# Mixture-of-experts stage: four split buffers in place of three, and a first gather in two steps

## The chip, the cores and the metric

The kernel runs on one core of one Trainium2 chip. The metric is the device time of one execution in microseconds (us), lower being better. Before the change the median of three runs is 1938.57 us (1936.62 to 1939.97).

## The reference, cut to what matters

Two layers of a hybrid backbone are computed for 256 latent tokens of width 1024 (and 256 context tokens). The change lies in the last part of the second layer: the output projection of its mixer, the router, and eight experts of which each token uses two.

```python
def moe_swiglu(xs, router_w, router_b, w_gate, w_up, w_down):
    logits = xs @ router_w + router_b
    top_val, top_idx = lax.top_k(logits, TOP_K)
    top_p = jax.nn.softmax(top_val, axis=-1)
    gates = jnp.sum(jax.nn.one_hot(top_idx, N_EXPERTS) * top_p[..., None], axis=-2)
    y = jnp.zeros_like(xs)
    for e in range(N_EXPERTS):
        y = y + gates[..., e:e + 1] * swiglu(xs, w_gate[e], w_up[e], w_down[e])
    return y
...
def swiglu(xs, w_gate, w_up, w_down):
    return (jax.nn.silu(xs @ w_gate) * (xs @ w_up)) @ w_down
```

D_MODEL is 1024, D_EXPERT 2816, N_EXPERTS 8 and TOP_K 2. The arithmetic is float32.

## The kernel before, in words

**Weights in two parts.** A float32 weight is used as the sum of a rounded part `hi` and a rest `lo`, each of a type that TensorE (PE) multiplies in one pass. A weight tile is 128 x 2048 numbers, 1 MB. The sync engine's queue (SP, L214) loads it into a buffer `raw`; ScalarE (ACT, L635) writes `hi` from it; VectorE (DVE, L636) writes `lo` as the difference; then PE multiplies with both. The three pools are opened by `open_ring` (L206, called at L1703): six buffers for `raw`, three for `hi`, three for `lo`. A buffer of `raw` is free when its `lo` is written, one of `hi` or `lo` when PE has read it.

**Experts.** The router sorts the experts by their number of tokens. Four of them (position 0 to 3) get 128 slots and are called big here, four get 64 slots and are called small; `order` in `experts` (L1503) takes big and small in turn. Each expert has 33 tiles: 11 of `m_gate`, 11 of `m_up`, 11 of `m_down`, in all 264 tiles. `expert_up` (L1586) goes through gate and up in six pieces of 512 hidden columns (the last 256). For a big expert each piece of a tile takes three matmuls (L1603, L1604, L1606); then come `h` (ACT L1632, DVE L1633), transposes (PE L1635) and `hT` (ACT L1639, DVE L1640). A small expert has the two halves of its input side by side in 128 columns, so two matmuls do (L1603, L1604), and sums over the halves (L1615 to L1629: ACT `h`, DVE `u`, PE L1619, ACT `g`, ...). `expert_down` (L1645) of the expert before is woven into the pieces, one tile at a time.

**Gather.** `gather` (L1543) makes the inputs of one big and one small expert at once. DVE writes a table of zeros and ones, `hot` (L1551, four instructions of 128 columns: two token blocks, two experts); PE multiplies the tokens with it (L1561, 32 matmuls of 256 columns, 128 for the big and 128 for the small expert); ACT copies the results of the first 16 (L1569) and DVE those of the other 16 (L1567) into `xghi`, `xglo` and `xs`; PE turns `hot` (L1574) and fetches the gate values (L1579), DVE copies them to `gslot` (L1582). The first gather comes right after the router, the next three at the third piece (`c == 2`) of each small expert. The router's last steps on DVE are the sort (up to L1481), the integers for the addresses of the experts' weights (L1487 to L1494), and the loading of one of them into registers of the engines (L1495).

**Before the router.** `odd_out` (L1187) projects the mixer's output with four tiles of `o_out`. They go through the same three pools, and the first three tiles of the experts are split in the same stage, ahead of need.

**Order.** Every engine works through its own list in the order that the compiled program fixes. So what an engine can do next is set by that list and by the waits of its head.

Of the kernel before, what the change touches and what calls it, by code (L numbers as in the profile page):

```python
# [162 lines left out]
class Kernel:  # L163
# [174 lines left out]

    def ssq_add(self, pool, tag, bank, m, segs, bufs=3, direct=False):
        nc = self.nc  # L340
        n = segs[-1][1]
        sq = pool.tile([P, T], F32, tag=tag, name="nsq", bufs=bufs)[:, :n]
        for a, b, v in segs:
            nc.scalar.activation(sq[:, a:b], v, AF.Square)
        if direct:
            for t in range(n // P):
                nc.tensor.matmul(bank[:, t:t + 1], lhsT=sq[:, t * P:t * P + P], rhs=self.mean_d[:, 0:1],
                                 start=m == 0 and t == 0, stop=m == KD - 1 and t == n // P - 1)
            return
# [837 lines left out]
    def odd_out(self, od):  # L1187
# [5 lines left out]
        cm = self.cm = self.const(self.mp, "moe")  # L1193
        self.sorted = self.mp.tile([P, 6, NE], F32, name="sorted")
        self.ints = self.mp.tile([P, 1 + 2 * NE], I32, name="ints")
        self.y2 = [flat[1][:, i * D:i * D + D] for i in range(2)]
        with ExitStack() as st:
# [28 lines left out]
            def back(m, ps):  # L1226
                r = self.resl[:, m]
                nc.vector.scalar_tensor_tensor(r, ps, mix[2][:, m, 0:1], r, op0=ALU.mult, op1=ALU.add)
                xm = yp.tile([P, L], F32, tag="xg", name="xg", bufs=3)
                nc.scalar.activation(xm, r, AF.Copy, scale=gs[:, m, 0:1])  # L1230
                self.ssq_add(yp, "sq", ssq, m, [(0, L, r)])
# [189 lines left out]
    def route(self, xp, lg, cm, tag):  # L1421
# [33 lines left out]
        for b in range(2):  # L1455
            mm(cnt, lhsT=self.ones, rhs=sel[:, b], start=b == 0, stop=b == 1)
        pg = tile_(6, NE)
        pos = pg[:, 0:2]
# [22 lines left out]
        nc.vector.tensor_reduce(self.sorted, moved, axis=AX.X, op=ALU.add)  # L1481
        self.pos, self.gate = self.sorted[:, 0:2], self.sorted[:, 2:4]
        over = tile_(NE)
        nc.vector.tensor_tensor(over, self.sorted[:, 5], cm["cap"], op=ALU.subtract)
        nc.vector.tensor_scalar(over, over, 0.0, None, op0=ALU.max)
        ints = xp.tile([P, 1 + 2 * NE], I32, name="ints")
        nc.vector.tensor_copy(ints[:, 1:1 + NE], self.sorted[:, 4])  # L1487
# [5 lines left out]
                                         max_val=NE - 1) for i in range(1, NE)]  # L1493
        nc.vector.tensor_copy(self.ints, ints)  # L1494
        self.most = nc.values_load(ints[0:1, 0:1], min_val=0, max_val=L)  # L1495
# [7 lines left out]
    def experts(self, wk):  # L1503
        got = {0: self.gather(wk, self.pos, 0, NB)}
        order = [p + NB * s for p in range(NB) for s in range(2)]
        down, todo = iter(()), None
        for n, p in enumerate(order):
            small, i = divmod(p, NB)
            x, hT = got[i][small], []
            for c, _ in enumerate(self.expert_up(wk, p, x, hT)):  # L1510
                if c == 0 and todo:
                    self.scatter(wk, *todo)
                    todo = None
                if c == 2 and small and i + 1 < NB:
# [12 lines left out]

    def overflow(self, wk):
        with self.tc.If(self.most > 0):
            for p in range(NE):  # L1530
                over = self.nc.values_load(self.ints[0:1, 1 + NE + p:2 + NE + p], min_val=0, max_val=L)
                with self.tc.If(over > 0):
                    pos = wk.tile([P, 2, NE], F32, tag="pos2", name="pos2", bufs=1)
                    self.nc.vector.tensor_scalar(pos, self.pos, float(-P if p < NB else -64), None, op0=ALU.add)
                    x, hT = self.gather(wk, pos, p, None)[0], []
                    for _ in self.expert_up(wk, p, x, hT, False):
                        pass
                    for todo in self.expert_down(wk, p, x, hT, False):
                        pass
                    self.scatter(wk, *todo)  # L1540
            self.finish(wk)

    def gather(self, wk, pos, p, s):  # L1543
        nc = self.nc
        mm = nc.tensor.matmul
        cm = self.cm
        hot = wk.tile([P, 2, 2, P], F32R, tag="hot", name="hot", bufs=2)
        both = [(1, p, "slot")] + ([] if s is None else [(0, s, "slot2")])
        for b in range(2):
            for i, e, slot in both:  # L1550
                nc.vector.tensor_scalar(hot[:, b, i], cm[slot], pos[:, b, e:e + 1], None, op0=ALU.is_equal)  # L1551
        xg = [wk.tile([P, KD, P], F32R, tag="xg" + n, name="xg" + n, bufs=1) for n in ("hi", "lo")]
        xs = None if s is None else wk.tile([P, KD, P], F32R, tag="xs", name="xs", bufs=2)
        cols = slice(0, 2) if xs is not None else slice(1, 2)
        for j, (src, dst) in enumerate(zip((self.thi, self.tlo), xg)):
            for k in range(0, KD, 2):
                ps = self.bank("tr").rearrange("p (k i w) -> p k i w", k=2, i=2)
                for kk in range(2):
                    c = slice((k + kk) * P, (k + kk + 1) * P)
                    for b in range(2):  # L1560
                        mm(ps[:, kk, cols], lhsT=src[:, b, c], rhs=hot[:, b, cols], start=b == 0, stop=b == 1)  # L1561
                parts = [(dst[:, k:k + 2], ps[:, :, 1])]
                if xs is not None:
# [13 lines left out]
        for i, e, _ in both:  # L1577
            for b in range(2):
                mm(ps[:, i:i + 1], lhsT=hot[:, b, i].bitcast(F32), rhs=self.gate[:, b, e:e + 1], start=b == 0,  # L1579
                   stop=b == 1)  # L1580
        gs = wk.tile([P, 2], F32, tag="gslot", name="gslot", bufs=2)
        nc.vector.tensor_copy(gs[:, cols], ps[:, cols])  # L1582
        big = (xg, hotT[:, 1], gs[:, 1:2])
        return [big] if xs is None else [big, ((xs,), hotT[:, 0], gs[:, 0:1])]

    def expert_up(self, wk, p, now, hT, ahead=True):  # L1586
# [4 lines left out]
        for c in range(6):  # L1591
# [21 lines left out]
            if small:  # L1613
                u = wk.tile([P, 512], F32, tag="u", name="u", bufs=2)
                nc.scalar.activation(h[:, :width], pgu[0][:, :width], AF.Copy)  # L1615
                nc.vector.tensor_copy(u[:, :width], pgu[1][:, :width])
                for i, t in enumerate((h, u)):
                    for j in range(n):
                        mm(ps[:, 256 * i + 64 * j:256 * i + 64 * j + 64], lhsT=t[:, j * P:(j + 1) * P],  # L1619
                           rhs=self.cm["sum2"], start=True, stop=True)  # L1620
                g = wk.tile([P, 256], F32, tag="g", name="g", bufs=2)[:, :64 * n]
                nc.scalar.activation(g, ps[:, :64 * n], AF.Silu)
                nc.vector.tensor_tensor(g, g, ps[:, 256:256 + 64 * n], op=ALU.mult)
                if c == 0:
                    self.hS = self.mp.tile([P, FT, 2, 64], F32R, tag="hS", name="hS", bufs=1)
                o = self.hS[:, 4 * c:4 * c + n]
# [58 lines left out]
    def run(self, inject=None):  # L1685
        self.setup()
        self.small = self.ctx.enter_context(self.pool("small"))
        with ExitStack() as st:
# [7 lines left out]
            with ExitStack() as s1:  # L1696
# [32 lines left out]
```

## Time and profile before

| | before |
|---|---|
| median of three runs | 1938.57 us |
| profiled execution, its own time | 1935.74 us |
| span of the profiled execution | 1933.9 us |
| PE busy, share of the span | 1768.6 us, 91% |
| DVE busy | 1445.9 us, 75% |
| ACT busy | 1006.3 us, 52% |
| mean granted clock of TensorE | 0.967 |

The profiled execution took 1.84 us more than its span, from the first to the last instruction. Busy time is a sum over the span; the stages have different limits, and the experts take the part from about 1125 us on. Windows of 198 us, 1392 to 1590 and 1590 to 1788, hold just one pair of experts each.

### The profile page before, as it was taken

How to read it: one execution, taken by the hardware profiler on the slowest of the kernel's cores; microseconds unless marked ns; L12 is line 12 of the kernel's file. 1: busy time of each engine (PE TensorE's matmuls, PEld its weight loads, DVE VectorE, ACT ScalarE, POOL GpSimd, SP SyncE). 2: the span in 40 equal slices, each digit the busy share in tenths (PEclk: the TensorE clock that was granted, in tenths of full speed). 3: DMA queues.
4: the chain of work that ended last, by engine and by line, in shares of the span. 5: the costliest groups of instructions: out<-in, count | busy, mean ns of one | idle time of the engine just before them, and what ended most of it. 6: DMA issues, size and time to landing. Idle time of an engine off the chain costs nothing.

```text
span 1933.9 us, 28843 instructions
## 1 busy us (share of the span) xinstructions
PE 1768.6 (91%) x11628; PEld 1390.4 (72%) x11628; DVE 1445.9 (75%) x1966; ACT 1006.3 (52%) x1131; POOL 90.3 (5%) x92
## 2 busy tenths in 40 slices
PE   6989999698999999989999879989999899998996
PEld 3657776377888888778876768777777677777775
DVE  4577888657995383456685678888888889888987
ACT  3433325635232222366562357776677677767774
POOL 0011102200000000002110000000000000000000
PEclk8999999798999999989999889999999999999997
DMA  7232111325666163123203339999999999989993
GB/s 291 91 111 88 46 42 49 109 88 200 236 238 239 66 223 125 66 80 109 87 23 146 144 133 359 363 344 363 345 341 363 353 346 341 370 335 360 352 380 119
DMA packets 57310, 409.32 MB, mean 212 GB/s; under 512 B 6480, under 2 KB 6864, under 8 KB 8016
## 3 DMA queue, kind: packets, MB, share of 16 engines
q1 hardware_dynamic: 57168, 407.39, 56.5%
q8 instruction: 93, 1.52, 0.3%
q14 instruction: 49, 0.40, 0.1%
HBM read 406.32 MB, written 1.05 MB: 211 GB/s over the span
## 4 chain that ended last, share of the span: by engine, by line
PE 71%; DVE 17%; ACT 7%; issue 4%; POOL 1%; DMA 0%; SPq 0%; DVEq 0%; ACTq 0%; POOLq 0%
DVE lo L636 10%; PE bank_gu L1604 6%; PE bank_b L234 6%; PE bank_b L235 6%; PE bank_b L236 6%; PE bank_gu L1603 5%; ACT hi L635 5%; PE bank_mm L234 4%; PE bank_mm L235 4%; PE bank_mm L236 4%; PE bank_gu L1606 3%; PE bank_dn L1660 3%; PE bank_dn L1659 2%; PE bank_dn L1662 1%; PE bank_tr L1619 1%
## 5 line engine op out<-in xcount | busy, mean ns | idle before, releaser
L636 DVE TENSOR_TENSOR lo<-raw,hi 128x2048 fp32r<-128x2048 f32 (+1 forms) x398 | 765.4, 1946 | 186.3 <-ACT hi L635 184.2
L635 ACT ACTIVATE hi<-raw 128x2048 fp32r<-128x2048 f32 (+1 forms) x398 | 641.3, 1632 | 276.0 <-PE bank_b L235 140.5
L1604 PE MATMUL bank_gu<-lo,xghi 128*128 128x512 f32 (+1 forms) x384 | 148.9, 388 | 27.2 <-DVE lo L636 26.7
L1604 PE MATMUL bank_gu<-lo,xs 128*128 128x512 f32 (+1 forms) x384 | 146.2, 387 | 7.5 <-DVE lo L636 6.4
L1603 PE MATMUL bank_gu<-hi,xghi 128*128 128x512 f32 (+1 forms) x384 | 145.6, 379 | 0.0
L1606 PE MATMUL bank_gu<-hi,xglo 128*128 128x512 f32 (+1 forms) x384 | 144.5, 376 | 0.0
L1603 PE MATMUL bank_gu<-hi,xs 128*128 128x512 f32 (+1 forms) x384 | 144.3, 382 | 0.2
L234 PE MATMUL bank_b<-xhi,hi 128*128 128x512 f32 x352 | 138.0, 394 | 2.9 <-ACT xhi L635 2.9
L234 PE MATMUL bank_mm<-xhi,hi 128*128 128x512 f32 (+1 forms) x320 | 120.9, 380 | 21.5 <-ACT hi L635 15.3
L235 PE MATMUL bank_b<-xlo,hi 128*128 128x512 f32 x352 | 137.9, 392 | 0.0
L236 PE MATMUL bank_b<-xhi,lo 128*128 128x512 f32 x352 | 137.6, 391 | 0.0
L236 PE MATMUL bank_mm<-xhi,lo 128*128 128x512 f32 (+1 forms) x320 | 118.3, 370 | 2.9 <-DVE lo L636 2.1
L235 PE MATMUL bank_mm<-xlo,hi 128*128 128x512 f32 (+1 forms) x320 | 119.7, 374 | 0.0
L1604 PEld LDWEIGHTS bank_gu<-lo,xghi 128*128 128x128 f32 x384 | 72.2, 188 | 54.0 <-DVE lo L636 41.6
L1604 PEld LDWEIGHTS bank_gu<-lo,xs 128*128 128x128 f32 x384 | 72.4, 188 | 32.6 <-DVE lo L636 21.2
L312 DVE SCALAR_TENSOR_TENSOR ada<-ada_raw,sT,ada 128x1024 f32<-128x1024 f32 x70 | 87.2, 1282 | 5.5 <-DMA ada_raw<-in_ada_v 4.8
L234 PEld LDWEIGHTS bank_mm<-xhi,hi 128*128 128x128 f32 x320 | 62.4, 196 | 37.2 <-ACT hi L635 16.5
L1603 PEld LDWEIGHTS bank_gu<-hi,xghi 128*128 128x128 f32 x384 | 72.3, 188 | 13.5
L1603 PEld LDWEIGHTS bank_gu<-hi,xs 128*128 128x128 f32 x384 | 72.4, 188 | 12.4 <-ACT hi L635 1.5
L1606 PEld LDWEIGHTS bank_gu<-hi,xglo 128*128 128x128 f32 x384 | 72.4, 188 | 12.2
L234 PEld LDWEIGHTS bank_b<-xhi,hi 128*128 128x128 f32 x352 | 66.5, 189 | 17.0 <-ACT xhi L635 3.2
L1660 PE MATMUL bank_dn<-lo,hT 128*128 128x512 f32 x176 | 72.8, 414 | 6.2 <-DVE lo L636 6.2
(512 smaller groups left out, 3461.0 us busy)
## 6 DMA issues: line engine op xcount, KB each, us to landing
raw<-in_m_up SPq DMA_DIRECT2D x88, 1024.0 KB, 7.2
raw<-in_m_gate SPq DMA_DIRECT2D x88, 1024.0 KB, 7.1
raw<-in_m_down SPq DMA_DIRECT2D x88, 1024.0 KB, 7.3
ada_raw<-in_ada_v SPq DMA_DIRECT2D x28, 1024.0 KB, 4.9
raw<-in_ada SPq DMA_DIRECT2D x20, 1024.0 KB, 6.0
raw<-in_o_in SPq DMA_DIRECT2D x16, 1024.0 KB, 4.9
raw<-in_w_in SPq DMA_DIRECT2D x12, 1024.0 KB, 4.9
raw<-in_f_gate SPq DMA_DIRECT2D x11, 1024.0 KB, 5.8
```

Of the source, the lines that this page charges most:

```text
L234: mm(out, lhsT=whi, rhs=xhi, start=start, stop=False)
L235: mm(out, lhsT=whi, rhs=xlo, start=False, stop=False)
L236: mm(out, lhsT=wlo, rhs=xhi, start=False, stop=stop)
L312: nc.vector.scalar_tensor_tensor(acc[r], w[:, k], s, acc[r], op0=ALU.mult, op1=ALU.add)
L635: self.nc.scalar.activation(hi, x, AF.Copy)
L636: (self.nc.gpsimd if pool else self.nc.vector).tensor_tensor(lo, x, hi.bitcast(F32), op=ALU.subtract)
L1603: mm(o, lhsT=xg[0][:, kk], rhs=whi(k), start=kk == 0, stop=False)
L1604: mm(o, lhsT=xg[0][:, kk], rhs=wlo(k), start=False, stop=small and kk == 7)
L1606: mm(o, lhsT=xg[1][:, kk], rhs=whi(k), start=False, stop=kk == 7)
L1619: mm(ps[:, 256 * i + 64 * j:256 * i + 64 * j + 64], lhsT=t[:, j * P:(j + 1) * P], rhs=self.cm["sum2"], start=True, stop=True)
L1659: mm(py[a], lhsT=h[0], rhs=whi(i)[:, half[a]], start=f == 0, stop=False)
L1660: mm(py[a], lhsT=h[0], rhs=wlo(i)[:, half[a]], start=False, stop=len(h) == 1 and f == FT - 1)
```

## The change

`open_ring` gets four buffers for `hi` and `lo` in place of three. To make room, several other tiles are taken less often or put elsewhere: `xs` goes into a tile that is no longer needed (`self.x[0]`), `hot`, `u` and `g` get one buffer, and the squares in `ssq_add` get a narrower tile. The first gather is cut in two: one for the first big expert alone, from the places before the sort (`self.plain`), and one for the first small expert from the sorted places. The copy of the integers (L1494 before) goes.

```diff
-    def ssq_add(self, pool, tag, bank, m, segs, bufs=3, direct=False):
+    def ssq_add(self, pool, tag, bank, m, segs, bufs=3, direct=False, width=T):
...
-        sq = pool.tile([P, T], F32, tag=tag, name="nsq", bufs=bufs)[:, :n]
+        sq = pool.tile([P, width], F32, tag=tag, name="nsq", bufs=bufs)[:, :n]
...
+        self.plain = self.mp.tile([P, 6, NE], F32, name="plain")
         self.ints = self.mp.tile([P, 1 + 2 * NE], I32, name="ints")
+        self.xs = [flat[0][:, i * D:i * D + D].rearrange("p (k w) -> p k w", k=KD) for i in range(2)]
...
-        pg = tile_(6, NE)
+        pg = self.plain
...
-        ints = xp.tile([P, 1 + 2 * NE], I32, name="ints")
+        ints = self.ints
...
-        nc.vector.tensor_copy(self.ints, ints)
         self.most = nc.values_load(ints[0:1, 0:1], min_val=0, max_val=L)
...
     def experts(self, wk):
-        got = {0: self.gather(wk, self.pos, 0, NB)}
+        got = {0: self.gather(wk, self.plain, 0, None)}
...
             x, hT = got[i][small], []
+            if n == 0:
+                got[0] += self.gather(wk, self.sorted, None, NB)
...
-                    got[i + 1] = self.gather(wk, self.pos, i + 1, NB + i + 1)
+                    got[i + 1] = self.gather(wk, self.sorted, i + 1, NB + i + 1)
...
-    def gather(self, wk, pos, p, s):
+    def gather(self, wk, places, p, s):
...
-        hot = wk.tile([P, 2, 2, P], F32R, tag="hot", name="hot", bufs=2)
-        both = [(1, p, "slot")] + ([] if s is None else [(0, s, "slot2")])
+        pos, gate = places[:, 0:2], places[:, 2:4]
+        hot = wk.tile([P, 2, 2, P], F32R, tag="hot", name="hot", bufs=1)
+        jobs = [(i, e, slot) for i, e, slot in ((1, p, "slot"), (0, s, "slot2")) if e is not None]
+        cols = slice(jobs[-1][0], jobs[0][0] + 1)
...
-        xs = None if s is None else wk.tile([P, KD, P], F32R, tag="xs", name="xs", bufs=2)
...
+        if s is not None:
+            xs = self.xs[s % 2]
...
-        hotT = wk.tile([P, 2, L], F32R, tag="hotT", name="hotT", bufs=2)
+        hotT = wk.tile([P, 2, L], F32R, tag="hotT", name="hotT", bufs=3)
...
-                u = wk.tile([P, 512], F32, tag="u", name="u", bufs=2)
+                u = wk.tile([P, 512], F32, tag="u", name="u", bufs=1)
...
-                g = wk.tile([P, 256], F32, tag="g", name="g", bufs=2)[:, :64 * n]
+                g = wk.tile([P, 256], F32, tag="g", name="g", bufs=1)[:, :64 * n]
...
-            self.open_ring(st, 6, 3, 2048)
+            self.open_ring(st, 6, 4, 2048)
```

**Steady work, ACT.** In the second big expert ACT's list, from one `hT` to the next, with the events that each instruction waits for (`PE` is a matmul, `DVE` an instruction of DVE, `DMAHW` a load); before:

```order
L1639 ACTIVATE hT_11220<-bank_tr_11326 128x512 [waits PE_49]
L635 ACTIVATE hi_11356<-raw_11354 128x2048 [waits DMAHW5_49,DVE_49]
L635 ACTIVATE hi_11374<-raw_11372 128x2048 [waits DMAHW6_49,DVE_49]
L635 ACTIVATE hi_11389<-raw_11387 128x2048 [waits DMAHW7_49,DVE_49,PE_49]
L1632 ACTIVATE h_11437<-bank_gu_11335 128x512 [waits PE_49]
L635 ACTIVATE hi_11407<-raw_11405 128x2048 [waits DMAHW0_49,DVE_49]
L635 ACTIVATE hi_11425<-raw_11423 128x2048 [waits DMAHW1_49,DVE_49,PE_49]
L635 ACTIVATE hi_11451<-raw_11449 128x2048 [waits DMAHW2_49,DVE_49,PE_49]
L1639 ACTIVATE hT_11445<-bank_tr_11438 128x512 [waits PE_49]
```

After the change the same place reads:

```order
L1649 ACTIVATE hT_11263<-bank_tr_11369 128x512 [waits PE_49]
L635 ACTIVATE hi_11399<-raw_11397 128x2048 [waits DMAHW5_49,DVE_49]
L635 ACTIVATE hi_11417<-raw_11415 128x2048 [waits DMAHW6_49,DVE_49]
L635 ACTIVATE hi_11432<-raw_11430 128x2048 [waits DMAHW7_49,DVE_49]
L1642 ACTIVATE h_11480<-bank_gu_11378 128x512 [waits PE_49]
L635 ACTIVATE hi_11450<-raw_11448 128x2048 [waits DMAHW0_49,DVE_49]
L635 ACTIVATE hi_11468<-raw_11466 128x2048 [waits DMAHW1_49,DVE_49]
L635 ACTIVATE hi_11494<-raw_11492 128x2048 [waits DMAHW2_49,DVE_49,PE_49]
L1649 ACTIVATE hT_11488<-bank_tr_11481 128x512 [waits PE_49]
```

The instructions stand in the same order and the `hi` between two others are of the same tiles; two of the three waits for PE by a `hi` are gone.

**First gather, PE.** From its last transposes on, PE's list before:

```order
L1574 MATMUL bank_tr_9856<-const_base_60,hot_9792 128x128 x3
L1606 MATMUL bank_gu_9870<-hi_9871,xglo_9798 128x512
L1579 MATMUL bank_tr_9863<-sorted_9211,hot_9792 128x1 [waits DVE_49,PE_49]
L1579 MATMUL bank_tr_9863<-sorted_9211,hot_9792 128x1 x3
L1603 MATMUL bank_gu_9870<-hi_9871,xghi_9797 128x512
L1604 MATMUL bank_gu_9870<-lo_9872,xghi_9797 128x512
L1606 MATMUL bank_gu_9870<-hi_9871,xglo_9798 128x512
```

And after, where the lines have moved by 8 to 10:

```order
L1584 MATMUL bank_tr_9843<-const_base_60,hot_9790 128x128
L1613 MATMUL bank_gu_9914<-hi_9915,xghi_9793 128x512
L1614 MATMUL bank_gu_9914<-lo_9916,xghi_9793 128x512
L1589 MATMUL bank_tr_9848<-plain_9212,hot_9790 128x1 [waits DVE_49]
L1589 MATMUL bank_tr_9848<-plain_9212,hot_9790 128x1
L1616 MATMUL bank_gu_9914<-hi_9915,xglo_9794 128x512
L1613 MATMUL bank_gu_9914<-hi_9915,xghi_9793 128x512
L1569 MATMUL bank_tr_9856<-hot_9853,xhi_4458 128x128 [waits DVE_49,Activation_49]
L1569 MATMUL bank_tr_9856<-hot_9853,xhi_4458 128x128 [waits DVE_49]
L1569 MATMUL bank_tr_9856<-hot_9853,xhi_4458 128x128 x2
L1569 MATMUL bank_tr_9862<-hot_9853,xhi_4458 128x128 x4
```

The first gather's 32 matmuls have 128 columns instead of 256, and after only four matmuls of the first gate tile a second run of 32 follows, for the small expert, with a table `hot` that DVE writes in between.

**Output projection, DVE.** What DVE does between the last normalisation of the mixer and the first results of the projection, before:

```order
L636 TENSOR_TENSOR lo_9301<-raw_9297,hi_9300 128x2048
L636 TENSOR_TENSOR lo_9376<-raw_9372,hi_9375 128x2048
L636 TENSOR_TENSOR lo_9452<-raw_9448,hi_9451 128x2048
L1206 TENSOR_TENSOR rwg_9224<-rw_9222,gs_9220 128x64
L1218 TENSOR_TENSOR rbias_9248<-bank_t_9239,par_58 128x8
L626 SCALAR_TENSOR_TENSOR xlo_4459<-bank_t_9250,hg_7054,xhi_4458 128x256
```

After (between the two pieces stand six more `xlo`, L626, without anything among them):

```order
L636 TENSOR_TENSOR lo_9302<-raw_9298,hi_9301 128x2048
L1208 TENSOR_TENSOR rwg_9225<-rw_9223,gs_9221 128x64
L1220 TENSOR_TENSOR rbias_9249<-bank_t_9240,par_58 128x8
L636 TENSOR_TENSOR lo_9377<-raw_9373,hi_9376 128x2048
L626 SCALAR_TENSOR_TENSOR xlo_4459<-bank_t_9251,hg_7054,xhi_4458 128x256
```

```order
L636 TENSOR_TENSOR lo_9453<-raw_9449,hi_9452 128x2048
L626 SCALAR_TENSOR_TENSOR xlo_4459<-bank_t_9286,hg_7054,xhi_4458 128x256
L636 TENSOR_TENSOR lo_9529<-raw_9525,hi_9528 128x2048
L1230 SCALAR_TENSOR_TENSOR resl_84<-bank_mm_9300,vec1_73,resl_84 128x256
```

Two `lo` that stood ahead of `rwg` now stand behind it, the third ahead of the last `xlo`, and the fourth (which stood behind the second `resl`) ahead of the first. Four tiles of the experts are split behind these, where three were; the last of them stands at the place where the last stood before.

## Rows read from the trace of the kernel before

**Rows 1.** The page: header and part 1, busy time.

```profile
span 1933.9 us, 28843 instructions
...
PE 1768.6 (91%) x11628; PEld 1390.4 (72%) x11628; DVE 1445.9 (75%) x1966; ACT 1006.3 (52%) x1131; POOL 90.3 (5%) x92
```

**Rows 2.** Windows: stretch, length, busy by engine, clock, DMA share, GB/s.

```profile
1135.00:1150.00 15.00, 15.00 (x68) 12.02 (x67) 10.62 (x8) 11.82 (x8) 0.00 (x0) 1.00 0.52 179
1150.00:1200.00 50.00, 50.00 (x249) 41.65 (x248) 44.62 (x27) 38.20 (x27) 0.00 (x0) 1.00 0.96 362
...
1392.00:1590.00 198.00, 183.37 (x887) 145.34 (x886) 173.25 (x126) 139.96 (x110) 0.00 (x0) 1.00 0.94 350
```

**Rows 3.** Waits, 1150 to 1934: us in total, times, longest us.

```profile
DVE lo L636 <- ACT hi L635: 72.9, 87, 2.4
...
PE bank_gu L1604 <- DVE lo L636: 33.0, 44, 2.7
...
ACT hi L635 <- PE bank_gu L1606: 25.8, 26, 3.9
...
ACT hi L635 <- PE bank_gu L1603: 11.6, 31, 1.2
```

**Rows 4.** Waits of the load queue, same stretch.

```profile
SPq L214 <- DVE lo L636: 487.4, 200, 6.2
```

**Rows 5.** Timeline of ACT and DVE, a small expert: start, us, engine, operation, idle before.

```profile
1450.64 0.60 ACT L1615 ACTIVATE h<-bank_gu 128x512 f32<-128x512 f32 x1 [1.28 <-PE bank_gu L1604]
1451.13 5.59 ACT L635 ACTIVATE hi<-raw 128x2048 fp32r<-128x2048 f32 x3
...
1453.07 6.70 DVE L636 TENSOR_TENSOR lo<-raw,hi 128x2048 fp32r<-128x2048 f32 x3 [1.35 <-ACT hi L635]
```

**Rows 6.** Timeline of ACT and PE, a big expert.

```profile
1344.94 0.60 ACT L1639 ACTIVATE hT<-bank_tr 128x512 fp32r<-128x512 f32 x1 [3.38 <-PE bank_tr L1635]
1345.44 5.51 ACT L635 ACTIVATE hi<-raw 128x2048 fp32r<-128x2048 f32 x3
...
1349.73 0.50 PE L1604 MATMUL bank_gu<-lo,xghi 128*128 128x512 f32 x1 [1.09 <-DVE lo L636]
```

**Rows 7.** Timeline of ACT and DVE at the last tiles.

```profile
1897.35 3.78 ACT L635 ACTIVATE hi<-raw 128x2048 fp32r<-128x2048 f32 x2 [1.27 <-PE bank_dn L1659]
...
1899.30 2.29 DVE L636 TENSOR_TENSOR lo<-raw,hi 128x2048 fp32r<-128x2048 f32 x1 [0.29 <-ACT hi L635]
```

**Rows 8.** Timeline of DVE and PE at the first gather.

```profile
1123.96 0.18 DVE L1494 COPY ints<-ints 128x17 int32<-128x17 int32 x1
1124.61 1.66 DVE L1551 TENSOR_SCALAR hot<-const_moe,sorted 128x128 fp32r<-128x128 f32 x8 [0.47 <-DVE ints L1494]
1125.24 4.00 PE L1561 MATMUL bank_tr<-hot,xhi 128*128 128x256 f32 x16 [6.46 <-DVE hot L1551]
...
1129.31 1.30 PE L1561 MATMUL bank_tr<-hot,xlo 128*128 128x256 f32 x8
...
1133.09 1.02 PE L1579 MATMUL bank_tr<-sorted,hot 128*128 128x1 f32 x8
```

**Rows 9.** Chain that ended last, a small expert: start, us, what.

```profile
1445.99 0.84 PE bank_tr L1619 x8
```

**Rows 10.** Timeline of DVE, PE and ACT in the output projection.

```profile
1068.01 6.69 DVE L636 TENSOR_TENSOR lo<-raw,hi 128x2048 fp32r<-128x2048 f32 x3
...
1074.97 1.11 PE L623 MATMUL bank_t<-const_base,yo 128*128 128x128 f32 x4 [0.69 <-DVE rbias L1218]
...
1105.34 1.91 ACT L635 ACTIVATE hi<-raw 128x2048 fp32r<-128x2048 f32 x1 [1.31 <-PE bank_mm L235]
...
1107.28 2.29 DVE L636 TENSOR_TENSOR lo<-raw,hi 128x2048 fp32r<-128x2048 f32 x1 [1.34 <-ACT hi L635]
```

**Rows 11.** Timeline of ACT, first small expert, third piece.

```profile
1216.49 0.60 ACT L1615 ACTIVATE h<-bank_gu 128x512 f32<-128x512 f32 x1 [1.08 <-PE bank_gu L1604]
...
1217.40 1.93 ACT L635 ACTIVATE hi<-raw 128x2048 fp32r<-128x2048 f32 x1
```

More of the change, by code (lines that the diff above doesn't have):

```diff
@@ L1230, in back @@
                 nc.scalar.activation(xm, r, AF.Copy, scale=gs[:, m, 0:1])
-                self.ssq_add(yp, "sq", ssq, m, [(0, L, r)])
+                self.ssq_add(yp, "sq", ssq, m, [(0, L, r)], width=L)
                 c = slice(m % 4 * P, m % 4 * P + P)
@@ L1481, in route @@
         nc.vector.tensor_reduce(self.sorted, moved, axis=AX.X, op=ALU.add)
-        self.pos, self.gate = self.sorted[:, 0:2], self.sorted[:, 2:4]
         over = tile_(NE)
@@ L1532, in overflow @@
                 with self.tc.If(over > 0):
-                    pos = wk.tile([P, 2, NE], F32, tag="pos2", name="pos2", bufs=1)
-                    self.nc.vector.tensor_scalar(pos, self.pos, float(-P if p < NB else -64), None, op0=ALU.add)
+                    pos = wk.tile([P, 4, NE], F32, tag="pos2", name="pos2", bufs=1)
+                    self.nc.vector.tensor_scalar(pos[:, 0:2], self.sorted[:, 0:2], float(-P if p < NB else -64), None,
+                                                 op0=ALU.add)
+                    self.nc.vector.tensor_copy(pos[:, 2:4], self.sorted[:, 2:4])
                     x, hT = self.gather(wk, pos, p, None)[0], []
@@ L1546, in gather @@
         cm = self.cm
-        hot = wk.tile([P, 2, 2, P], F32R, tag="hot", name="hot", bufs=2)
-        both = [(1, p, "slot")] + ([] if s is None else [(0, s, "slot2")])
+        pos, gate = places[:, 0:2], places[:, 2:4]
+        hot = wk.tile([P, 2, 2, P], F32R, tag="hot", name="hot", bufs=1)
+        jobs = [(i, e, slot) for i, e, slot in ((1, p, "slot"), (0, s, "slot2")) if e is not None]
+        cols = slice(jobs[-1][0], jobs[0][0] + 1)
         for b in range(2):
-            for i, e, slot in both:
+            for i, e, slot in jobs:
                 nc.vector.tensor_scalar(hot[:, b, i], cm[slot], pos[:, b, e:e + 1], None, op0=ALU.is_equal)
-        xg = [wk.tile([P, KD, P], F32R, tag="xg" + n, name="xg" + n, bufs=1) for n in ("hi", "lo")]
-        xs = None if s is None else wk.tile([P, KD, P], F32R, tag="xs", name="xs", bufs=2)
-        cols = slice(0, 2) if xs is not None else slice(1, 2)
-        for j, (src, dst) in enumerate(zip((self.thi, self.tlo), xg)):
+        xg = xs = None
+        if p is not None:
+            xg = [wk.tile([P, KD, P], F32R, tag="xg" + n, name="xg" + n, bufs=1) for n in ("hi", "lo")]
+        if s is not None:
+            xs = self.xs[s % 2]
+        for j, src in enumerate((self.thi, self.tlo)):
             for k in range(0, KD, 2):
@@ L1561, in gather @@
                         mm(ps[:, kk, cols], lhsT=src[:, b, c], rhs=hot[:, b, cols], start=b == 0, stop=b == 1)
-                parts = [(dst[:, k:k + 2], ps[:, :, 1])]
+                parts = []
+                if xg:
+                    parts.append((xg[j][:, k:k + 2], ps[:, :, 1]))
                 if xs is not None:
@@ L1570, in gather @@
         ps = self.bank("tr").rearrange("p (i b w) -> p i b w", i=2, b=2)
-        hotT = wk.tile([P, 2, L], F32R, tag="hotT", name="hotT", bufs=2)
-        for i, _, _ in both:
+        hotT = wk.tile([P, 2, L], F32R, tag="hotT", name="hotT", bufs=3)
+        for i, _, _ in jobs:
             for b in range(2):
@@ L1576, in gather @@
         ps = self.bank("tr")
-        for i, e, _ in both:
+        for i, e, _ in jobs:
             for b in range(2):
-                mm(ps[:, i:i + 1], lhsT=hot[:, b, i].bitcast(F32), rhs=self.gate[:, b, e:e + 1], start=b == 0,
+                mm(ps[:, i:i + 1], lhsT=hot[:, b, i].bitcast(F32), rhs=gate[:, b, e:e + 1], start=b == 0,
                    stop=b == 1)
-        gs = wk.tile([P, 2], F32, tag="gslot", name="gslot", bufs=2)
+        gs = wk.tile([P, 2], F32, tag="gslot", name="gslot", bufs=3)
         nc.vector.tensor_copy(gs[:, cols], ps[:, cols])
-        big = (xg, hotT[:, 1], gs[:, 1:2])
-        return [big] if xs is None else [big, ((xs,), hotT[:, 0], gs[:, 0:1])]
+        now = ((xg, p), ((xs,), s))
+        return [(x, hotT[:, i], gs[:, i:i + 1]) for (x, e), i in zip(now, (1, 0)) if e is not None]
     def expert_up(self, wk, p, now, hT, ahead=True):
@@ L1624, in expert_up @@
                 if c == 0:
-                    self.hS = self.mp.tile([P, FT, 2, 64], F32R, tag="hS", name="hS", bufs=1)
+                    self.hS = wk.tile([P, FT, 2, 64], F32R, tag="hS", name="hS", bufs=1)
                 o = self.hS[:, 4 * c:4 * c + n]
```

## The prediction

> **What bounds the kernel now.** I read the header and the busy times first [rows 1]: TensorE (PE) is busy for 1768.6 of 1933.9 us, but that is a sum over stages, so I went to windows of the stage that the four buffers serve [rows 2]. From 1135 to 1200 us PE has no pause at all (15.00 of 15.00, 50.00 of 50.00): there PE alone sets the pace. In the window 1392 to 1590, one big and one small expert, PE works 183.37 of 198 us and VectorE (DVE) 173.25; 14.63 us of PE are idle. Loads move 350 GB/s. Are they the limit? No: the load queue itself waits, 487.4 us in 200 waits, for `lo` to free a buffer of `raw` [rows 4], so loads run as far ahead as the six `raw` buffers let them, and the change leaves those at six.
>
> Next the list of waits [rows 3]. PE waits 33.0 us for `lo`, DVE's `lo` waits 72.9 us for ScalarE's (ACT's) `hi`, and `hi` waits 25.8 and 11.6 us for a matmul that still reads the buffer it wants. Taken alone this reads as a chain in which three buffers are too few. So I looked at what stands ahead of the `hi` that PE in the end waits for. In a small expert [rows 5] ACT waits 1.28 us for PE's last gate matmul, writes `h` from 1450.64, and the next `hi` starts at 1451.13, at the end of `h`; 1.94 us later, at 1453.07, `lo` starts, after 1.35 us in which DVE waited for just this `hi`. In a big expert [rows 6] ACT waits 3.38 us for PE's transposes, writes `hT` from 1344.94, and `hi` starts at 1345.44, with its `lo` and then PE late by 1.09 us at 1349.73. In both, `hi` is late because it stands behind `h` or `hT` in ACT's list, and those need PE's newest result. No buffer is waited for there. I followed the true predecessors back in this way, through the lists and the trace, over the whole of the experts; only one `hi` that waits for a buffer lies on the path: that at 1897.35, by 1.27 us [rows 7].
>
> **The four buffers.** The order printed above shows ACT's list in the steady part: same instructions, same order, same tiles; two of three waits of `hi` for PE go. The `hi` behind `hT` and behind `h` had no such wait before either. So the loop PE, `hT` (or `h`), `hi`, `lo`, PE keeps its length in each piece, and what is saved elsewhere on ACT is spent waiting for `h` or `hT`. I take 0 for the steady part. At the last tiles the 1.27 us wait goes, but behind it DVE had been idle for only 0.29 us before its `lo` at 1899.30 [rows 7] and runs on without a gap, so 0.3 is gained, at most 1.3. In the first small expert, at the third piece, the list does change: `hi` started at 1217.40, behind `h` (1216.49, 0.60 us) and two copies of the second gather [rows 11]; after the change a pair of copies has moved behind it. It could start some 0.1 us ahead of the end of `h`, as in [rows 5], at 1216.98, 0.4 earlier; with what DVE's list loses of such copies there I take 0.6, from 0 to 1.5.
>
> **The first gather.** It starts earlier. DVE copied the integers at 1123.96 and then sat 0.47 us idle at the register load, so that `hot` began at 1124.61 [rows 8]; now `hot` stands where that copy stood, 0.65 us earlier. Two tables of 0.2 us each (8 in 1.66) need to be ready, not four: 0.4 more. That is 1.05 us. What is added is 32 matmuls of 128 columns for the small expert. The trace shows no run of such. Those with 64 columns take 0.105 us each (8 in 0.84 [rows 9]), those with 256 columns 0.16 with the copies that they wait for (8 in 1.30 [rows 8]); since 256 columns and 64 lie so near, I do not count the first 32 as cheaper for having 128 columns now. The second 32 cost 3.4 to 5.2 us; I take 0.13 each, 4.15. Transposes and gate values are as many as before, only in two halves. The new `hot` waits until PE has read the old one (one buffer now); DVE then needs about 0.5 us for the small copy and two tables, and the two gate matmuls that stand between cover most of it. Sum: +3.1 us, from +0.3 (waits for copies in the first 32 fall by 1 us, since ACT has only half the copies to make, and no other gap comes) to +5.2 (no earlier start). Nothing hides it: PE does not pause from 1135 to 1200 [rows 2], so what is added ahead of that moves everything behind.
>
> The Trainium skill says in "TensorE: Matmul & The Clock Gate", section "Back-to-back issue gap", that the spacing of matmuls in a stream of weight loads and matmuls is set by both, and gives 81 ns for 128 columns. By that the 32 would cost an estimated 2.6 us and the whole would come out 1.5 us lower; the row with 64 columns, at 0.105 us [rows 9], is already slower than that page's figure, so the rows decide.
>
> **The output projection.** Two `lo` (3 take 6.69 us) move from ahead of `rwg` to behind it. PE waited 0.69 us for what follows [rows 10], so no more than that is gained. Against it one `lo` of 2.29 us now stands ahead of the last `xlo`, and the last matmuls of the first group need that; PE has the other group's matmuls to do meanwhile. One more expert tile is split here, but the `hi` at 1105.34 that waited for the projection's last reads and its `lo` at 1107.28, which is on the path to the router, stand where they stood [rows 10]. I take +0.4, from -0.7 to +2.3.
>
> **Sum.** 0.4 + 3.1 - 0.6 - 0.3 = +2.6 us. Against the profiled execution that makes 1935.74 + 2.6 = 1938.3 us; this execution lies 2.8 us under the median of the runs, so for a median I add to that: 1938.57 + 2.6 = 1941.2 us. That is 0.13% and under what a measurement of this kernel can tell from no change, about 0.2% (3.9 us). The bounds: -0.7 + 0.3 - 1.5 - 1.3 = -3.2 and 2.3 + 5.2 = +7.5, so 1935.4 to 1946.1. The other edits (narrower squares, `u` and `g` with one buffer, `xs` elsewhere, the register load of `most` after the experts) I cost at nothing. `u` and `g` are read by PE or DVE a whole piece before the next is written. The late register load stands behind the last output instruction of its engine, beside the final store.
>
> **Rivals.** *The waits for buffers are the limit after all: faster.* For it speak the 37.4 us that ACT waits for them and the 14.63 us that PE loses in each of four pairs, 58.5 us in all [rows 2, 3]. If half of ACT's waits came off the path: 1938.57 - 19 = 1920 us; all: 1901. Against it: rows 5 and 6, where the late `hi` waits for no buffer [rows 5, 6]. It would need the waits that go to lie on the path at most pieces. The Trainium skill has this rival as a rule: "Perfetto Trace Analysis", section "Optimization Strategy", says that the same gap repeating on the engine that should be saturated can mean too little SBUF or PSUM for the next tile (buffer count, tile sizes). The gap before PE's `lo` matmul does repeat, but the trace names another cause. Chance 0.14.
>
> *The second gather is slower than I think: slower.* The first 16 matmuls took 4.00 us, 0.25 each [rows 8], at a low clock and with waits for copies. If the second 32 go at that rate they cost 8.0 us, 3.85 more than I take: 1945.0 us. It decides from (3.9 + 1.05 + 0.5) / 32 = 0.17 us per matmul (0.5 being what the other terms give back), just above the 0.16 of the eight. Chance 0.12 in this form; the upper part of my own bounds reaches past +3.9 too.
>
> *Nothing at all:* the second gather falls into time that PE loses further on, since from about 1216 us a loop through ACT and DVE sets the pace. Against it: that loop begins with PE's gate matmul [rows 11], so it moves with PE. It gives 1938 us. Chance 0.06.
>
> **Numbers.** My own sum gets 0.68: 0.44 under +3.9, 0.20 over it, 0.04 under -3.9 by things that I have not seen. With the rivals: faster 0.14 + 0.04 = 0.18, within 0.2% 0.44 + 0.06 = 0.50, slower 0.20 + 0.12 = 0.32. The range 1930 to 1947 us takes in my bounds, the slow rival, and the small end of the fast one; it leaves out most of that rival's 0.14 and a little above.
>
> **What would show it.** In the changed profile the windows of a pair of experts should hold 198 us again with PE busy 183. The waits of `hi` for `bank_gu` should shrink to a few us, those of `h` and `hT` for PE grow, and PE's 33.0 us for `lo` stay. The first matmul of the gather should come about 1 us earlier against the sort, the second gather's gate values some 3 us later than 1133.09 with fewer gate matmuls done. I am wrong if the pair takes 193 us or less, if the second gather runs at 0.17 us per matmul or more, or if the projection's last `hi` moves by over 2 us.

## The result and the profile after

The changed kernel takes 1947.53 us (median of five runs, 1946.79 to 1951.45) against 1938.57 us before in the same call: a ratio of 1.0051 with a 95% interval of 1.0038 to 1.0063. It is slower by 9 us. The prediction was +2.6 us, and 1947.53 lies just above its range.

The profiled execution took 1950.07 us, one of the two slower of the five, so its span is 14.4 us longer than that of before [rows 1], not 9. The page of after, header and busy time:

```profile
span 1948.3 us, 28886 instructions
...
PE 1783.5 (92%) x11660; PEld 1404.7 (72%) x11660; DVE 1445.3 (74%) x1966; ACT 999.5 (51%) x1132; POOL 90.1 (5%) x92
```

PE has 32 more matmuls and 15 us more busy time, which would be 0.47 us for each of them; so others have become longer too. The steady part is not where this lies. The window of one pair of experts, moved along with the span, and the waits from 1150 to 1950 us (us in total, times, longest):

```profile
1408.00:1606.00 198.00, 183.23 (x887) 144.80 (x886) 174.03 (x129) 138.12 (x110) 0.00 (x0) 1.00 0.94 350
```

```profile
ACT hT L1649 <- PE bank_tr L1645: 70.9, 23, 4.0
ACT g L1632 <- PE bank_tr L1629: 65.9, 24, 4.5
...
PE bank_gu L1614 <- DVE lo L636: 33.0, 44, 2.7
...
ACT hi L635 <- PE bank_gu L1616: 20.4, 14, 4.5
...
ACT hi L635 <- PE bank_gu L1613: 0.9, 1, 0.9
```

Two lines of the same list before, 1150 to 1934:

```profile
ACT hT L1639 <- PE bank_tr L1635: 54.8, 22, 3.4
ACT g L1622 <- PE bank_tr L1619: 45.3, 24, 2.8
```

PE's share of the 198 us is that of [rows 2], and its wait for `lo` is 33.0 us in 44 waits, as in [rows 3]. Of the 37.4 us in which `hi` waited for a buffer 21.3 are left (17.0 if the stretch is moved along with the span), and ACT's waits for PE's transposes grew: `hT` from 54.8 to 70.9 us, `g` from 45.3 to 65.9. The wait only changed its name.

The loss lies at the first gather. PE's timeline of after, from the start of the gather:

```profile
1128.18 3.64 PE L1569 MATMUL bank_tr<-hot,xhi 128*128 128x128 f32 x16 [5.49 <-DVE hot L1557]
1131.62 3.62 PE L1569 MATMUL bank_tr<-hot,xlo 128*128 128x128 f32 x16
...
1138.05 3.51 PE L1569 MATMUL bank_tr<-hot,xhi 128*128 128x128 f32 x16
1141.35 3.62 PE L1569 MATMUL bank_tr<-hot,xlo 128*128 128x128 f32 x16
...
1150.33 0.63 PE L1616 MATMUL bank_gu<-hi,xglo 128*128 128x512 f32 x1
```

and windows of the same stretch (after the length: busy time of PE, weight load, DVE, ACT and GpSimd, then the granted clock):

```profile
1128.00:1132.00 4.00, 3.82 (x18) 3.85 (x19) 0.23 (x2) 1.29 (x4) 0.00 (x0) 0.50 0.00 0
1132.00:1136.00 4.00, 4.00 (x20) 3.90 (x20) 1.70 (x4) 0.47 (x2) 0.00 (x0) 0.50 0.00 0
...
1144.00:1148.00 4.00, 4.00 (x16) 3.69 (x16) 1.52 (x7) 0.38 (x1) 0.00 (x0) 0.50 0.00 0
1148.00:1152.00 4.00, 4.00 (x13) 3.10 (x13) 0.34 (x1) 1.91 (x1) 0.00 (x0) 0.64 0.00 0
1152.00:1156.00 4.00, 4.00 (x19) 3.23 (x18) 1.95 (x1) 2.82 (x3) 0.00 (x0) 1.00 0.22 47
```

PE is busy without a pause, and yet its granted clock is 0.50, 1.2 GHz, until about 1150.9 us: 22.7 us from the first matmul. Before, the clock rose 3.7 us after the first matmul, at 1128.9:

```profile
1128.00:1129.00 1.00, 1.00 (x7) 1.00 (x7) 0.00 (x0) 0.48 (x3) 0.00 (x0) 0.55 0.00 0
1129.00:1135.00 6.00, 6.00 (x41) 5.22 (x41) 3.34 (x13) 1.28 (x4) 0.00 (x0) 1.00 0.01 3
```

The eight matmuls from 1129.31 then took 1.30 us, 0.16 each [rows 8]; after the change all 64 take 0.22 us each (16 in 3.5 to 3.6), and a gate matmul of 512 columns takes 0.43 from one start to the next instead of 0.23. From the first table `hot` to the 15th gate matmul it is 1150.33 - 1127.76 = 22.6 us; before it was 1135.91 - 1124.61 = 11.3. That makes 11.3 of the 14.4 us. From that matmul to the end both executions take 798.0 us.

The other 3.1 us lie ahead of the gather: 3.0 more in the output projection and 1.0 more before it starts, less 0.8 by which `hot` now comes earlier behind the router's norm. DVE in the projection of after, with its wait (idle before, and its cause):

```profile
1074.19 0.17 DVE L1220 TENSOR_TENSOR rbias<-bank_t,par 128x8 f32<-128x8 f32 x1 [2.80 <-PE bank_t L1218]
1074.30 2.29 DVE L636 TENSOR_TENSOR lo<-raw,hi 128x2048 fp32r<-128x2048 f32 x1
...
1080.39 2.28 DVE L636 TENSOR_TENSOR lo<-raw,hi 128x2048 fp32r<-128x2048 f32 x1
1082.59 0.48 DVE L626 SCALAR_TENSOR_TENSOR xlo<-bank_t,hg,xhi 128x256 fp32r<-128x256 f32 x1
```

The `lo` that moved behind `rbias` now waits with it: DVE is idle for 2.80 us, in which it wrote `lo` before [rows 10]. From the first matmul of the stage (1067.69 before, 1068.65 after) to `mcol`, the first instruction of the router's norm (1109.49 and 1113.40), it takes 41.80 us before and 44.75 after.

### The profile page after: what moved, and what is told of

Read it like the earlier page. It is cut to its first block, busy times and chain, and to the rows that moved or that the text cites. A ratio compares the mean times of both kernels' runs of the same rounds, so it can differ in the third digit from the quotient of the medians.

```text
span 1948.3 us, 28886 instructions
## 1 busy us (share of the span) xinstructions
PE 1783.5 (92%) x11660; PEld 1404.7 (72%) x11660; DVE 1445.3 (74%) x1966; ACT 999.5 (51%) x1132; POOL 90.1 (5%) x92
## 3 DMA queue, kind: packets, MB, share of 16 engines
HBM read 406.32 MB, written 1.05 MB: 209 GB/s over the span
## 4 chain that ended last, share of the span: by engine, by line
PE 73%; DVE 14%; ACT 6%; issue 4%; DMA 2%; POOL 1%; SPq 0%; DVEq 0%; ACTq 0%; POOLq 0%
DVE lo L636 7%; PE bank_gu L1614 7%; PE bank_b L234 6%; PE bank_b L235 6%; PE bank_b L236 6%; PE bank_gu L1613 6%; ACT hi L635 4%; PE bank_mm L234 4%; PE bank_mm L235 4%; PE bank_mm L236 4%; PE bank_gu L1616 3%; PE bank_dn L1670 3%; PE bank_dn L1669 3%; PE bank_tr L1569 1%; PE bank_dn L1672 1%
## 5 line engine op out<-in xcount | busy, mean ns | idle before, releaser
L635 ACT ACTIVATE hi<-raw 128x2048 fp32r<-128x2048 f32 (+1 forms) x398 | 634.3, 1629 | 252.0 <-PE bank_b L235 132.8
L1614 PE MATMUL bank_gu<-lo,xhi 128*128 128x512 f32 (+1 forms) x384 | 145.5, 385 | 7.7 <-DVE lo L636 6.4
L1613 PE MATMUL bank_gu<-hi,xhi 128*128 128x512 f32 (+1 forms) x384 | 143.4, 380 | 0.3
L1614 PEld LDWEIGHTS bank_gu<-lo,xhi 128*128 128x128 f32 x384 | 72.3, 188 | 32.5 <-DVE lo L636 21.2
L1613 PEld LDWEIGHTS bank_gu<-hi,xhi 128*128 128x128 f32 x384 | 72.4, 189 | 12.2 <-ACT hi L635 1.6
```

Of the source, the lines that this page charges most:

```text
L635: self.nc.scalar.activation(hi, x, AF.Copy)
L1613: mm(o, lhsT=xg[0][:, kk], rhs=whi(k), start=kk == 0, stop=False)
L1614: mm(o, lhsT=xg[0][:, kk], rhs=wlo(k), start=False, stop=small and kk == 7)
```

## The experiments

Theory A: in the split gather the matmuls of 128 columns leave TensorE at the low clock, and that is most of the loss. Theory B: the fourth buffer costs it, by the output projection and what follows. Theory C: it is the 32 added matmuls as such. Ratios below are to the kernel before in the same call, with 95% intervals.

**Four buffers, gather in one step.** The edit to the changed kernel:

```diff
-        got = {0: self.gather(wk, self.plain, 0, None)}
+        got = {0: self.gather(wk, self.sorted, 0, NB)}
...
-            if n == 0:
-                got[0] += self.gather(wk, self.sorted, None, NB)
```

> The changed kernel with the first gather in one step again (both experts, 256 columns, sorted places), four buffers kept. Theory A (in the split gather the matmuls of 128 columns leave TensorE at the low clock, so that gather and the first gate matmuls run at half speed until about 1150 us): the clock rises again some 4 us after the gather starts, and the time falls from 1947.5 to 1938 to 1943 us, the rest over the kernel before being the output projection. Theory B (the fourth buffer costs the time, through the new order in the output projection and the waits behind it): it stays at 1945 us or more.

1938.29 us, ratio 0.9997 (0.9986 to 1.0008). In the windows the clock comes up again, about 5.5 us after the first matmul at 1123.40:

```profile
1127.00:1129.00 2.00, 2.00 (x10) 1.90 (x10) 0.14 (x1) 0.83 (x4) 0.00 (x0) 0.50 0.00 0
1129.00:1131.00 2.00, 2.00 (x16) 1.88 (x14) 1.67 (x6) 0.00 (x0) 0.00 (x0) 0.99 0.00 0
```

So four buffers alone, with the other edits, neither gain nor lose what can be measured; the split is what costs.

**Three buffers, gather in two steps.** The edit to the changed kernel:

```diff
-            self.open_ring(st, 6, 4, 2048)
+            self.open_ring(st, 6, 3, 2048)
```

> The changed kernel with three buffers instead of four, the first gather in two steps kept. Theory A: it stays slow, 1943 to 1949 us, and the granted clock is 0.50 from the first matmul of the gather until well into the first gate tile. Theory B: it goes back to the time of the kernel before, 1937 to 1941 us.

1946.29 us, ratio 1.0035 (1.0022 to 1.0048). The clock is 0.50 from the first matmul at 1126.84 to about 1147.0, 20.2 us:

```profile
1127.00:1146.00 19.00, 19.00 (x84) 18.36 (x84) 4.24 (x16) 3.41 (x10) 0.00 (x0) 0.50 0.00 1
1146.00:1148.00 2.00, 2.00 (x8) 1.64 (x7) 0.11 (x1) 0.18 (x1) 0.00 (x0) 0.75 0.00 0
```

Theory B falls as the main cause. The 0.16% between three and four buffers here is within the intervals.

**First step at 256 columns.** The same weight loads, the same number of matmuls, twice the columns; what the added columns give is not used:

```diff
-            for i, e, slot in jobs:
+            for i, e, slot in jobs + ([(0, p, "slot2")] if s is None and places is self.plain else []):
...
-                        mm(ps[:, kk, cols], lhsT=src[:, b, c], rhs=hot[:, b, cols], start=b == 0, stop=b == 1)
+                        w = slice(0, 2) if places is self.plain else cols
+                        mm(ps[:, kk, w], lhsT=src[:, b, c], rhs=hot[:, b, w], start=b == 0, stop=b == 1)
```

> The changed kernel with the first step of the gather at 256 columns again: the second half of the columns is a table for the same expert in the other half, and its results are not used. Theory A (columns per matmul decide whether the clock rises): more columns, less time, 1939 to 1943 us, with the clock at 1.00 before the second step begins. Theory C (it is only the 32 added matmuls, at what a weight load costs): no gain, 1947 to 1949 us.

1941.11 us, ratio 1.0016 (1.0005 to 1.0027): by the medians 6.4 us less than the changed kernel, for doing more. PE's timeline, and windows:

```profile
1125.34 3.98 PE L1570 MATMUL bank_tr<-hot,xhi 128*128 128x256 f32 x16 [5.68 <-DVE hot L1557]
1129.12 1.86 PE L1570 MATMUL bank_tr<-hot,xlo 128*128 128x256 f32 x8
1131.05 1.19 PE L1570 MATMUL bank_tr<-hot,xlo 128*128 128x256 f32 x8
...
1133.90 2.13 PE L1570 MATMUL bank_tr<-hot,xhi 128*128 128x128 f32 x16
1135.95 2.16 PE L1570 MATMUL bank_tr<-hot,xlo 128*128 128x128 f32 x16
```

```profile
1126.00:1130.00 4.00, 4.00 (x20) 4.00 (x20) 0.00 (x0) 1.54 (x4) 0.00 (x0) 0.50 0.00 0
1130.00:1131.00 1.00, 1.00 (x6) 1.00 (x6) 0.42 (x1) 0.00 (x0) 0.00 (x0) 0.60 0.00 0
```

The first 16 take a little longer than 16 of 128 columns did in after (3.98 against 3.64 us): at the low clock the added 128 columns cost 0.02 us per matmul. But the clock is up by 1131, and the second step then takes 0.13 us per matmul instead of 0.22. Theory C falls as the main cause: the number of matmuls is that of after. The Trainium skill, "TensorE: Matmul & The Clock Gate", section "Why this matters for your kernels", advises for thin matmuls (a small M, the rows of the result) to do all tiles of the summed dimension K in a row or to pad M, since otherwise the clock goes up and down at every tile of K. Padding paid here too, 6.4 us for 32 wider matmuls; but PE had no pause in this stretch and its clock did not go up and down, so these runs do not show the page's reason.

**Matmuls ahead of the split gather.** Before the first `gather`, into a bank that nothing reads:

```diff
+        ps = self.bank("dn")
+        for _ in range(18):
+            self.nc.tensor.matmul(ps, lhsT=self.thi[:, 1, 512:640], rhs=self.thi[:, 1, 512:1024], start=True, stop=True)
```

> The changed kernel with 18 matmuls of 512 columns ahead of the first gather, into a bank that nothing reads, while TensorE waits for the sort. Theory A: the clock is 1.00 when the gather starts, each of its 64 matmuls takes 0.11 to 0.13 us, and the time falls by 8 to 12 us, to 1935.5 to 1939.5 us. Theory B: 1946 us or more, since the gather was not what cost the time.

1942.52 us, ratio 1.0017 (1.0006 to 1.0029): 5.0 us gained by the medians, 6.6 by the ratios, where 8 to 12 were expected, so the size was missed. PE's timeline shows what is left:

```profile
1120.15 6.46 PE L1506 MATMUL bank_dn<-xhi 128*128 128x512 f32 x18
1126.45 2.20 PE L1572 MATMUL bank_tr<-hot,xhi 128*128 128x128 f32 x16
1128.68 2.29 PE L1572 MATMUL bank_tr<-hot,xlo 128*128 128x128 f32 x16
...
1132.82 2.13 PE L1572 MATMUL bank_tr<-hot,xhi 128*128 128x128 f32 x16
1134.87 2.16 PE L1572 MATMUL bank_tr<-hot,xlo 128*128 128x128 f32 x16
```

At the full clock the second 32 still cost 4.3 us (2.13 + 2.16), which is my 4.15 of the prediction. The run is 4.2 us above the one with one step, and 0.29% or 5.6 us above the one with one step and the same matmuls ahead of it (below): both things are real, the clock and the added matmuls.

**The second step moved behind two pieces of gate and up.** The call goes inside the loop over the pieces:

```diff
-            if n == 0:
-                got[0] += self.gather(wk, self.sorted, None, NB)
...
+                if c == 2 and n == 0:
+                    got[0] += self.gather(wk, self.sorted, None, NB)
```

> The changed kernel with the second step of the gather moved to the third piece of the first big expert, so that gate matmuls of 512 columns follow the first step at once. Theory A: the clock rises within some 5 us of those, long before 20 us after the start, and the second step's 32 matmuls then take 0.13 us each: 1941 to 1944 us, 4 to 6 us less than the changed kernel, 3 to 5 more than with one step. Theory C (only the number of matmuls counts): 1947 us.

1944.34 us, ratio 1.0029 (1.0018 to 1.0039), just above what was expected. The clock now rises at about 1140.1, 5.3 us after the first gate matmul (1134.82) and 12.4 us after the gather's first; the second step begins at 1155.03 at the full clock, with pauses of 0.83 and 0.23 us for copies of ACT and DVE. In its last eight matmuls the clock falls again, at about 1160.6, and is back at 1167.5; that may be why the time lies above the forecast, but only this execution was profiled:

```profile
1155.00:1160.00 5.00, 4.16 (x29) 3.39 (x27) 4.79 (x4) 3.29 (x6) 0.00 (x0) 1.00 1.00 393
1160.00:1162.00 2.00, 1.78 (x11) 1.79 (x11) 0.78 (x4) 0.00 (x0) 0.00 (x0) 0.66 1.00 397
1162.00:1166.00 4.00, 4.00 (x14) 3.40 (x13) 1.10 (x6) 0.39 (x1) 0.00 (x0) 0.50 0.72 279
1166.00:1170.00 4.00, 4.00 (x16) 3.21 (x15) 1.48 (x1) 2.01 (x2) 0.00 (x0) 0.82 0.00 0
```

**Taking the clock out elsewhere.** Five further runs: the same kind of matmuls, with the lines shown above, with four buffers and one step (18); in the kernel before (20); with four buffers, one step and 20 more ahead of the output projection; and three buffers with one step, without and with 15 of them. The edit ahead of the output projection:

```diff
+            ps = self.bank("mm")
+            for _ in range(20):
+                mm(ps, lhsT=flat[0][:, :P], rhs=flat[0][:, :512], start=True, stop=True)
```

> Four buffers, the first gather in one step, and 18 matmuls of 512 columns ahead of it as in the run before with the split gather. Theory A: the gather starts at the full clock, its first 16 matmuls take 2.2 instead of 4.1 us, and the time is 2 to 3.5 us under that of the same kernel without them: 1935 to 1936.5 us. If the low clock at the gather cost nothing by itself: 1938 us as without.

1936.39 us, ratio 0.9988 (0.9976 to 1.0000).

> The kernel before with 20 such matmuls ahead of its gather and nothing else. Theory A: 2 to 3.5 us under the kernel before, 1934.5 to 1936.5 us. Beside the run with four buffers it shows what the four buffers are worth with the clock taken out: by my reading nothing in the experts, and 3 us lost in the output projection.

1933.54 us, ratio 0.9979 (0.9969 to 0.9989), a little more gained than expected. With the clock taken out three buffers stand 0.09% better than four, 1.7 us, as the 2 us lost in the output projection (net of the earlier `hot`) let one expect; their intervals overlap.

> As four buffers with one step and 18 matmuls ahead of the gather, and 20 more ahead of the output projection, where TensorE also waits for DVE and its clock falls to 0.50 until about 1080 us. If TensorE's clock is what bounds the start of that stage too: 1931 to 1934 us. If DVE's four lo and the copies bound it: 1935 to 1936.5 us, as without.

1936.63 us, ratio 0.9997 (0.9983 to 1.0010): no gain. The clock did rise, but the stage then waits for DVE, as in

```profile
1078.48 0.44 PE L623 MATMUL bank_t<-const_base,yo 128*128 128x128 f32 x2 [1.30 <-DVE xlo L626]
```

> The changed kernel with three buffers and the first gather in one step: what is left of the change is the storage of the smaller tiles and the copy of the integers that goes. It closes the square of three or four buffers and one or two steps. By the runs so far: within 2 us of the kernel before, rather 0.8 us under it (the table for the gather begins 0.8 us earlier behind the router), 1935 to 1938.5 us; the stretch from the first transposes of the output projection to the norm of the router's input takes 41.8 to 43.3 us, as in the other runs with three buffers, against 44.7 to 45.1 us with four.

1938.62 us, ratio 0.9999 (0.9986 to 1.0012), just above what was expected. It closes the square: one step 0.9999 with three buffers and 0.9997 with four, two steps 1.0035 and 1.0051. The projection took 42.1 us here, 41.8 to 43.3 in all five profiles with three buffers, 44.7 to 45.1 in the six with four where nothing was added ahead of it.

> The same with 15 matmuls of 512 columns ahead of the gather (fewer than 20, since those ended some 0.5 us behind the table). If what the two runs with such matmuls gained is the clock: 2 to 4 us under the run without them of this call, 1932 to 1935 us, and under the kernel before by more than 0.2%.

1933.78 us, ratio 0.9980 (0.9965 to 0.9995): 4.8 us under the run without them, where 2 to 4 were expected. Windows of its added matmuls and the start of its gather:

```profile
1116.00:1118.00 2.00, 2.00 (x6) 1.55 (x5) 2.00 (x10) 0.00 (x0) 0.00 (x0) 0.50 0.00 0
1118.00:1120.00 2.00, 2.00 (x8) 1.60 (x7) 1.83 (x8) 0.00 (x0) 0.00 (x0) 0.79 0.00 0
1120.00:1122.00 2.00, 1.49 (x9) 1.02 (x9) 1.34 (x9) 0.00 (x0) 0.00 (x0) 1.00 0.00 0
```

This run and the kernel before with 20 matmuls, both with three buffers, one step and the matmuls in PE's wait for the sort, beat both kernels, the one before by 0.2% with intervals that stay below 1.

The marks behind the differences, from the timelines of the profiles (us; first matmul of the projection, `mcol`, first `hot`, 15th gate matmul, span):

```
                       project.  mcol     hot      gate 15  span     proj.->mcol  hot->gate 15
before                 1067.69   1109.49  1124.61  1135.91  1933.9   41.8         11.3
after                  1068.65   1113.40  1127.76  1150.33  1948.3   44.8         22.6
4 buffers, one step    1063.35   1108.43  1122.78  1134.74  1934.0   45.1         12.0
3 buffers, two steps   1068.76   1112.06  1126.41  1148.09  1949.4   43.3         21.7
first at 256 columns   1065.67   1110.38  1124.73  1140.92  1938.7   44.7         16.2
warm, two steps        1066.29   1111.02  1125.36  1140.07  1939.2   44.7         14.7
warm, kernel before    1065.42   1108.71  1123.83  1134.28  1932.6   43.3         10.5
warm, 3 buffers        1064.30   1106.19  1120.54  1130.58  1930.3   41.9         10.0
```

## Why the prediction was wrong, step by step

**The four buffers, 0 in the steady part: right.** The pair of experts keeps its 198 us, PE's wait for `lo` stays at 33.0 us, and the run with four buffers and one step equals the kernel before. The reason given, that the late `hi` stands behind `h` and `hT` in ACT's list, fits the waits that took over. Only the size was off: I expected the buffer waits to shrink to a few us, and 21.3 are left. The 0.3 and 0.6 us at the last tiles and in the first small expert are too small to be told from the scatter.

**The start, 1.05 us earlier: right.** From `mcol` to the gather's first matmul it was 15.75 us before (1125.24 - 1109.49), and is 14.78 after (1128.18 - 1113.40): 0.97 earlier.

**The second 32 matmuls, "3.4 to 5.2 us; I take 0.13 each": this step failed.** They took 6.7 us (1138.05 to 1144.77, where the transposes start), 0.21 each. The price of 0.13 is right at the full clock: the two runs where it was up measured 0.13. What was wrong was to take the durations of rows 8 and 9 over from a stretch where PE had the full clock, as if the clock would rise in the changed stretch as it did before. I read the low clock as something that the first 16 matmuls pass through, and the change narrowed the very matmuls during which it rose. So not only the added 32 cost more: the second half of the first 32 and the gate matmuls up to 1150.9 ran at half speed too, none of which was a term of the sum. In place of +3.1, which counts the earlier start, it was +10.5 in the profiled execution (11.3 from `hot` on, less 0.8 by which `hot` came earlier), of which the run at 256 columns takes back 6.4 in the median.

The prediction also says that the trace shows no run of 128 columns. It does show one, at the start of the output projection, mostly at a granted clock of 0.50:

```profile
1067.69 3.56 PE L1211 MATMUL bank_t<-const_base,vec 128*128 128x128 f32 x16 [4.64 <-DVE tnsq L648]
```

That is 0.22 us each, and at this price the second 32 come to 7.1 us, though nothing in that row tells for how long the clock would stay low at the gather. The lower bound of this term does not come out of what is named for it either: 3.4 - 1.05 - 1 is +1.35, not +0.3; this changes nothing here.

**The rival "the second gather is slower than I think" had the sign and the place**, and its point of decision, 0.17 us per matmul, was passed. It had the low clock in its argument, but as a rate of those matmuls alone, not as something that the split prolongs for all that follows, and got 0.12.

**The output projection, +0.4: too small.** It measured +3.0 in the profile (1.4 to 3.3 between all profiles with three and with four buffers), beyond the 2.3 that I allowed; the last `hi` came 40.6 us after the first matmul instead of 37.7, over the 2 us that I named as a sign of being wrong. The 0.69 us that I let it gain did not come: DVE waits 2.80 us for PE at `rbias` with a `lo` behind it, so the `lo` are not moved into idle time but past it. The medians show less of it: four buffers stand 0.16% above three with two steps, 0.09% with one step and the clock taken out, and 0.02% below with one step, all within the intervals. That the `lo` are the cause is argued from the lists; that the clock is not was shown by the 20 matmuls ahead of the projection.

Whether the clock came up sooner in those three of the five runs that lie near 1947 us is open: one execution of after was profiled, and the runs with two steps differ by 2.5 us in it (20.2 and 22.7).

## What to carry to other kernels

Before you price an added or narrowed matmul, look up the granted clock of its stretch and what PE did before the clock rose there: here a stream with half the columns per matmul went with 1.2 GHz for 20 us and more, where the same number of matmuls at 256 columns in the first half had 2.4 GHz after 5.5. A wait on a buffer is worth a buffer only if the instruction that waits is late because of it; compare the lists of before and after, and look at what stands ahead of the late one. Where PE waits anyway and its clock has fallen, matmuls that nothing reads, ended just as the real work is ready, can pay: here 0.2%.

## What the runs showed of the hardware

A PE that is busy without a pause, by the profile 100% in every window from 1130 to 1150 us, stayed at a granted clock of 0.50 throughout 64 matmuls of 128 columns; with 256 columns in the first half the clock was 1.00 after 5.5 us. In the run with 18 matmuls of 512 columns ahead of the two steps, the same 64 ran at 1.00 throughout (1126 to 1140 us).

The columns are not all of it. The 16 matmuls of 128 columns at the start of the output projection, just as long (0.22 us each) but with float32 operands, bring no such stretch: in all eleven profiles where nothing was added ahead of them the clock is up 3.2 to 4.3 us after the first. In the kernel before:

```profile
1067.00:1070.00 3.00, 2.31 (x11) 2.31 (x12) 2.86 (x4) 0.06 (x1) 0.00 (x0) 0.50 1.02 415
1070.00:1071.00 1.00, 1.00 (x7) 1.00 (x7) 1.00 (x2) 0.54 (x1) 0.00 (x0) 0.56 0.72 303
1071.00:1074.00 3.00, 2.87 (x27) 2.63 (x25) 3.00 (x2) 1.36 (x4) 0.00 (x0) 1.00 0.92 322
```

What in the two streams makes the difference was not tested.

The clock also falls for some 3 us at single places in the experts, in some profiles and not in others. The time of a run goes with its mean granted clock: of 84 runs of the kernel before (1933 to 1944 us) the six fastest had 0.967 to 0.970, the six slowest 0.960 to 0.962. That these places are what lowers it is not shown. Windows of the run with three buffers and one step, at the change from one pair of experts to the next:

```profile
1300.00:1310.00 10.00, 7.30 (x32) 5.75 (x31) 9.58 (x10) 4.27 (x3) 0.00 (x0) 0.83 0.76 259
1500.00:1510.00 10.00, 7.30 (x30) 5.62 (x29) 9.57 (x10) 4.12 (x4) 0.00 (x0) 0.84 0.75 268
1700.00:1710.00 10.00, 7.30 (x28) 5.63 (x27) 9.06 (x10) 4.00 (x3) 0.00 (x0) 0.83 0.74 258
```

In the profile of the kernel before the clock is 1.00 at all three changes, though PE pauses there as long (2.70 us at the first change in both). What decides it was not tested.
